# Two products of 512 and 256 columns in place of three of 256, and both halves of an input tile side by side

## The chip, the cores and the metric

The kernel runs on one core of one Trainium2 chip. The metric is the device time of one execution in microseconds (us). TensorE (PE in the rows; PEld is its weight load) multiplies matrices into PSUM banks, VectorE (DVE) and ScalarE (ACT) work on tiles elementwise, GpSimd (POOL) does little here, and SyncE (SP) issues the loads.

## What is computed

One layer of a diffusion backbone over 256 latent tokens (`x`) with 256 context tokens (`ctx`), width 2048, in float32. The part that the change touches is the modulated norm and the start of the combined input projection:

```python
qa, ka, va, qb, kb, vb, rb, gf, gb, gate_a, gate_b = proj(modulate(x, g_mix[l], mod_x[0], mod_x[1]))
cqa, cka, cva, cqb, ckb, cvb, crb, cgf, cgb, cgate_a, cgate_b = proj(
    modulate(ctx, g_mix[l], mod_c[0], mod_c[1]))

def modulate(x, g, shift, scale):
    return rms_norm(x, g) * (1 + scale) + shift
```

`proj` multiplies by `w_in` (2048 rows, 13,344 columns) and splits the columns. The 1024 columns of `qb` are wanted of the latent tokens alone; `kb` and `vb` of both. After that come gated linear attention, windowed attention, the merge and a ConvFFN, which the change leaves as they are except for where some tiles lie.

## The kernel before

**Products in three parts.** A float32 factor is split in two: `hi` is the factor rounded to the matmul's type, `lo` is the rest. A product is then the sum of three matmuls: `hi` with `hi`, `hi` with `lo`, and `lo` with `hi`. For the weights, `wsplit` loads two K tiles (256 rows) by 512 columns into `raw`, ACT writes `whi` (line 220) and DVE subtracts to get `wlo` (line 221). Three such pairs of tiles are alive at a time: a new `whi` or `wlo` waits until TensorE is done with the one three steps back. A "step" below is one such pair of K tiles.

**The input.** The 16 K tiles of the normed input (`h`) are made in five groups as the modulation arrives: `GROUPS = [(0, 2), (2, 2), (4, 4), (8, 4), (12, 4)]` (first tile, number), called group 0 to group 4 here. `affine_shift` writes `hi` with ACT and `lo` with DVE (lines 543 and 546). They lie in four tiles `h0hi` to `h3hi` and four `h0lo` to `h3lo`, each with latent and context tokens of four K tiles.

**The loop over groups** (line 650 on). For each group from group 1 on it runs four column blocks: two query blocks of 512 columns (`QB0` and `QB1` here, `proj_T`, latent tokens only), a key block (`KB`, `proj_T` over both kinds of tokens, 512 columns of `h` a product) and a value block (`VA`, `proj_nat`). Each block sums its K tiles in PSUM banks (`acc`, a pool of four) and then adds the banks to an accumulator in SBUF (`qb0`, `kb0`, `va0`) with DVE at line 555. `KB` and `VA` use four banks; a query block uses two, each with two outputs of 256 columns. A bank of the next block but one, or of the next block where that uses all four, waits until its add is done. A group has one step (group 1) or two (groups 2 to 4) for each block.

**What stands between the blocks.** In groups 1 to 3 the modulation of the next group is worked out in between: `pm` products on loads named `mraw`, a transpose on DVE (`mtr`), `pcol` products, and small DVE operations on `scale`, `shift` and `xr`. In group 4 there are none. TensorE's order is that of the program up to the end of group 3; in group 4 the scheduler orders the instructions by its own reckoning of when each is ready. After group 4 come the `plr` products of a low-rank projection, four transposes `ptr`, 16 small products `plb`, and the rest of the layer.

**Later use of the tiles.** The context halves of the eight `h` tiles hold other data later: the natural-order input, the inner results `g`, and the attention's output.

Of the kernel before, what the change touches and what calls it, by code (L numbers as in the profile page):

```python
# [32 lines left out]
def layer_kernel(ctx, tc, A, out):  # L33
# [238 lines left out]
    def proj_T(w, c0, kts, rhs, evac, mid=None, fresh=False, by_tile=False):  # L272

        wide = rhs[0] is h_both
        per = 1 if wide else 2
        banks = [acc.tile([P, 512], F32, name="acc", tag="acc") for _ in range(4 // per)]
        for k0 in kts[::2]:
# [4 lines left out]
            for part in range(2):  # L282
                if whole and part:
                    break
                if part:
                    (mid or midway)()
                todo = [(f, k, x) for f in range(4) for k in range(nk) for x in range(2 - part)]
                if fresh and part == 0:
                    todo = [(f, k, x) for x in range(2) for k in range(nk) for f in range(4)]
                if whole:  # L290
                    todo = [(f, k, x) for f in range(4) for x in range(3) for k in range(nk)]
                end = None
                for f, k, x in todo:
                    kt = k0 + k
                    low = part == 1 or x == 2
                    w_ = (lo if low else hi)[:, k, f * P:(f + 1) * P]
                    b = f % per
                    o = banks[f // per]
                    if wide:
                        o = o.rearrange("p (s t) -> p s t", s=2)  # L300
                    else:
                        o = o[:, b * T:(b + 1) * T]
                    if whole and f == 2 and x + k == 0:
                        midway()
                    i = mm(o, w_, rhs[0](kt)[x % 2], start=(kt == kts[0] and b == 0 and not low and x == 0),
                           stop=(kt == kts[-1] and low), skip_group_check=True).ins
                    if whole and end is not None:
                        in_order(end, i)
                    end = i
# [199 lines left out]
    def h_tok(s, t):  # L509
        return lambda kt: (hh[kt // 4][:, s, kt % 4, t * P:(t + 1) * P],  # L510
                           hl[kt // 4][:, s, kt % 4, t * P:(t + 1) * P])

    def h_all(s):
        return lambda kt: (hh[kt // 4][:, s, kt % 4, :], hl[kt // 4][:, s, kt % 4, :])

    def h_both(kt):
        return hh[kt // 4][:, :, kt % 4, :], hl[kt // 4][:, :, kt % 4, :]
# [20 lines left out]
    def affine_shift(s, t0, n, behind=None):  # L538
        for kt in range(t0, t0 + n):
            xk = xr[2 * s + kt // 8][:, kt % 8, :]  # L540
            sh = shift1[:, s, kt:kt + 1]
            hi, lo = hh[kt // 4][:, s, kt % 4, :], hl[kt // 4][:, s, kt % 4, :]
# [15 lines left out]
    hh, hl = [], []  # L558

    def more_h(half):  # L560
        for q in (2 * half, 2 * half + 1):
            hh.append(M(f"h{q}hi", [P, 2, 4, T], F32R))
            hl.append(M(f"h{q}lo", [P, 2, 4, T], F32R))
# [86 lines left out]
    for gi, (t0, n) in enumerate(groups):  # L650
# [40 lines left out]
        for s in range(2):  # L691
# [371 lines left out]
    def natural(step):  # L1063
        raw = fetched.pop(step)
        e = step % 2
        if step >= KT // 2:
            a = S.activation(hh[e][:, 1], raw, AF.Copy).ins
            in_order(last_hi[0], a)
            in_order(last[0], a)
            a = V.tensor_tensor(hl[e][:, 1], raw, hh[e][:, 1].bitcast(F32), op=ALU.subtract).ins  # L1070
# [12 lines left out]
        split(hh[e][:, 1], hl[e][:, 1], raw)  # L1083
# [79 lines left out]
    def all_values():  # L1163
# [3 lines left out]
        def inner(step):  # L1167
            e = step % 2
            ax, ac = pair_x[step // (KT // 2)], pair_c[step // (KT // 2)]
            hn = (hh[e][:, 1], hl[e][:, 1])  # L1170
# [10 lines left out]
            for k in range(2):  # L1181
                split(hh[2 + e][:, 1, 2 * k:2 * k + 2, :], hl[2 + e][:, 1, 2 * k:2 * k + 2, :], gb[k])

        def outer(step, i, w):
# [4 lines left out]
            gs = [g[2 + e][:, 1].rearrange("p (k h) t -> p k h t", h=2) for g in (hh, hl)]  # L1189
# [85 lines left out]
    def attend(g, qT, qr):  # L1275
        for t in range(2):
# [53 lines left out]
            split(hh[g][:, 1, :, t * P:(t + 1) * P], hl[g][:, 1, :, t * P:(t + 1) * P],  # L1330
# [65 lines left out]
    for j in range(4):  # L1396
# [6 lines left out]
        proj_nat(A["w_attn_o"][0], 0, j * 512, ALL, [h_tok(1, 0), h_tok(1, 1)], at_evac)  # L1403
# [246 lines left out]
```

## Time and profile before

| what | before |
|---|---|
| median of 3 runs (lowest, highest) | 1936.68 us (1936.21, 1939.33) |
| the profiled execution | 1936.14 us |
| its span, first to last instruction | 1934.4 us |
| TensorE busy | 99% of the span |
| VectorE, ScalarE, GpSimd busy | 75%, 52%, 3% |
| mean granted TensorE clock | 0.999 of full speed |
| DMA over the span | 232 GB/s, all 16 engines busy in the first 96 us |

The profiled execution lasts 1.7 us longer than its span and lies 0.54 us under the median. The groups 1 to 4 take the stretch from 46 to 195 us of the span. A matmul's row gives a start and a modelled duration that overlaps with the next one, so what a matmul costs in a stream is the distance of the starts.

### The profile page before, as it was taken

To read this page: it belongs to the slowest core of one execution; us is meant where nothing else is said; L and a number is where in the kernel's file an instruction comes from. 1 tells how busy PE (TensorE), PEld (TensorE's weight loads), DVE (VectorE), ACT (ScalarE), POOL (GpSimd) and SP (SyncE) were. 2 spreads that over 40 slices of the span, in tenths; PEclk is the share of its full clock that TensorE was granted. 3 is DMA by queue.
4 is the path that set the end of the run, shared out by engine and by line. 5 is a ranking of instruction groups with operands and counts; after the bars stand their busy time and mean duration, and the time that the engine had idled before them with its cause. 6 is when DMAs were issued, how large, how long until landed. Compare 5 with 4: busy or idle time off the path is not lost.

```text
span 1934.4 us, 26471 instructions
## 1 busy us (share of the span) xinstructions
PE 1918.6 (99%) x9858; PEld 1595.9 (83%) x9858; DVE 1446.8 (75%) x2241; ACT 1007.7 (52%) x1469; POOL 51.2 (3%) x81
## 2 busy tenths in 40 slices
PE   8999999999999999999999999999999999999999
PEld 6678888888888887788888888888888888888887
DVE  5656767989787767898888776998886556777654
ACT  5223566666344456655544455755565334555532
POOL 0010110000100000000000000000000000000000
PEclk9999999999999999999999999999999999999999
DMA  9985325878976764457999987688886566666663
GB/s 396 413 304 147 94 66 186 247 253 270 321 241 214 236 186 120 128 182 226 347 344 350 349 278 221 206 279 277 282 268 218 193 194 186 189 192 186 198 214 109
DMA packets 194528, 450.24 MB, mean 233 GB/s; under 512 B 13776, under 2 KB 18128, under 8 KB 188512
## 3 DMA queue, kind: packets, MB, share of 16 engines
q1 hardware_dynamic: 187568, 428.13, 67.0%
q0 software_dynamic: 2912, 10.82, 1.6%
q10 hardware_dynamic: 3920, 9.61, 1.3%
q8 instruction: 77, 1.26, 0.3%
q14 instruction: 51, 0.42, 0.1%
HBM read 435.86 MB, written 12.65 MB: 232 GB/s over the span
## 4 chain that ended last, share of the span: by engine, by line
PE 95%; DMA 3%; DVE 1%; ACT 0%; issue 0%; SPq 0%; ACTq 0%
PE acc L84 70%; PE accs L84 13%; PE pg L84 4%; PE pa L96 2%; DMA raw<-in_w_in 1%; PE poa L96 1%; PE pS L96 1%; DMA mraw<-in_w_mod 1%; PE pm L96 1%; DMA xr<-in_ctxT 1%; PE ptp L99 1%; DVE wlo L221 0%; PE pto L99 0%; DMA pack<-in_k_pack 0%; PE plr L646 0%; PE pz L96 0%
## 5 line engine op out<-in xcount | busy, mean ns | idle before, releaser
L220 ACT ACTIVATE whi<-raw 128x1024 fp32r<-128x1024 f32 x568 | 601.3, 1060 | 732.7 <-PE acc L84 501.7
L221 DVE TENSOR_TENSOR wlo<-raw,whi 128x1024 fp32r<-128x1024 f32 x568 | 693.8, 1223 | 351.2 <-ACT whi L220 328.3
L84 PE MATMUL accs<-h,whi 128*128 128x512 f32 x704 | 244.5, 392 | 0.0
L84 PE MATMUL acc<-h,whi 128*128 128x512 f32 x640 | 222.3, 392 | 0.0
L84 PE MATMUL accs<-h,wlo 128*128 128x256 f32 x704 | 196.0, 278 | 0.0
L84 PE MATMUL acc<-h,wlo 128*128 128x256 f32 x640 | 178.1, 278 | 0.0
L84 PEld LDWEIGHTS accs<-h,whi 128*128 128x128 f32 x704 | 131.8, 187 | 29.8
L84 PEld LDWEIGHTS acc<-h,whi 128*128 128x128 f32 x640 | 119.8, 187 | 27.0
L84 PE MATMUL acc<-whi,ah 128*128 128x512 f32 x352 | 137.1, 389 | 0.0
L84 PE MATMUL acc<-whi,al 128*128 128x512 f32 x352 | 137.0, 389 | 0.0
L84 PEld LDWEIGHTS accs<-h,wlo 128*128 128x128 f32 x704 | 132.6, 188 | 0.0
L84 PEld LDWEIGHTS acc<-h,wlo 128*128 128x128 f32 x640 | 120.6, 188 | 0.1
L84 PE MATMUL acc<-whi,h2hi 128*128 128x512 f32 x256 | 101.1, 395 | 0.1
L84 PE MATMUL acc<-whi,h2lo 128*128 128x512 f32 x256 | 99.9, 390 | 0.9 <-DVE h2lo L63 0.9
L84 PE MATMUL acc<-whi,th 128*128 128x512 f32 x256 | 100.5, 393 | 0.0
L84 PE MATMUL acc<-whi,h3hi 128*128 128x512 f32 x256 | 100.2, 392 | 0.0
L84 PE MATMUL acc<-whi,h3lo 128*128 128x512 f32 x256 | 99.9, 390 | 0.0
L84 PE MATMUL acc<-whi,tl 128*128 128x512 f32 x256 | 99.7, 389 | 0.0
L84 PE MATMUL acc<-wlo,ah 128*128 128x512 f32 x352 | 94.2, 389 | 0.0
L403 DVE CUSTOM_DVE_ANT_0 raw<-raw,csrow,pack 128x1024 f32<-128x1024 f32 x64 | 81.8, 1278 | 0.0
L84 PEld LDWEIGHTS acc<-wlo,ah 128*128 128x128 f32 x352 | 66.1, 188 | 13.8
L84 PEld LDWEIGHTS acc<-whi,al 128*128 128x128 f32 x352 | 66.1, 188 | 13.7
(390 smaller groups left out, 3596.7 us busy)
## 6 DMA issues: line engine op xcount, KB each, us to landing
raw<-in_w_in SPq DMA_DIRECT2D x204, 512.0 KB, 4.4
raw<-in_w_up SPq DMA_DIRECT2D x176, 512.0 KB, 4.4
raw<-in_w_modT SPq DMA_DIRECT2D x128, 512.0 KB, 4.7
raw<-in_w_down SPq DMA_DIRECT2D x88, 512.0 KB, 4.0
mraw<-in_w_mod SPq DMA_DIRECT2D x32, 1024.0 KB, 14.0
raw<-in_w_attn_o SPq DMA_DIRECT2D x32, 512.0 KB, 5.8
raw<-in_w_gla_o SPq DMA_DIRECT2D x32, 512.0 KB, 5.8
raw<-in_w_out SPq DMA_DIRECT2D x32, 512.0 KB, 5.9
```

Source lines behind the costliest of these rows:

```text
L84: r = pe_seq(PE.matmul(*a, **k))
L96: return pe_seq(after(PE.matmul(*a, **k)))
L99: return pe_seq(after(PE.transpose(*a)))
L220: j = S.activation(hi[:, 0:n, :], raw[:, 0:n, :], AF.Copy).ins
L221: i = V.tensor_tensor(lo[:, 0:n, :], raw[:, 0:n, :], hi[:, 0:n, :].bitcast(F32), op=ALU.subtract).ins
L403: i0 = V.tensor_tensor_reduce(out=raws[i], in0=raws[i], in1=row[0], scale=1.0, scalar=d if h else bmod[:, b0:b0 + 1], op0=ALU.mult, op1=AL ...
```

## The change

The eight `h` tiles now hold two K tiles each, with `hi` and `lo` of a K tile next to each other, so that 512 columns of one product can run over both (`h_pair`). In the query blocks of groups 1 to 4, `whi` is multiplied with those 512 columns at once, and `wlo` with the 256 of `hi`. An output then takes a whole bank, 256 columns for `hi` and 256 for `whi` with `lo`, so that a query block has four banks, and `q_sums` adds each bank with two DVE additions of 256 columns. Group 0 stays as it was. The later users of the context halves address them through `half_of`, in the same shapes.

```diff
     def proj_T(w, c0, kts, rhs, evac, mid=None, fresh=False, by_tile=False):
 
         wide = rhs[0] is h_both
-        per = 1 if wide else 2
+        pair = rhs[0] is h_pair
+        per = 1 if wide or pair else 2
         banks = [acc.tile([P, 512], F32, name="acc", tag="acc") for _ in range(4 // per)]
...
-                todo = [(f, k, x) for f in range(4) for k in range(nk) for x in range(2 - part)]
+                todo = [(f, k, x) for f in range(4) for k in range(nk) for x in range(1 if pair else 2 - part)]
                 if fresh and part == 0:
-                    todo = [(f, k, x) for x in range(2) for k in range(nk) for f in range(4)]
+                    todo = [(f, k, x) for x in range(1 if pair else 2) for k in range(nk) for f in range(4)]
...
-                    else:
+                    elif not pair:
                         o = o[:, b * T:(b + 1) * T]
+                    elif low:
+                        o = o[:, 0:T]
...
-                    i = mm(o, w_, rhs[0](kt)[x % 2], start=(kt == kts[0] and b == 0 and not low and x == 0),
+                    i = mm(o, w_, rhs[0](kt)[part if pair else x % 2], start=(kt == kts[0] and b == 0 and not low and x == 0),
...
+    def h_pair(kt):
+        return hp[kt // 2][:, 0, kt % 2, :, :].rearrange("p i t -> p (i t)"), hp[kt // 2][:, 0, kt % 2, 0, :]
+
+    def half_of(i, q):
+        return hp[4 * i + q][:, 1].rearrange("p k i t -> p (k i) t")
...
-    hh, hl = [], []
+    hp = []
 
     def more_h(half):
-        for q in (2 * half, 2 * half + 1):
-            hh.append(M(f"h{q}hi", [P, 2, 4, T], F32R))
-            hl.append(M(f"h{q}lo", [P, 2, 4, T], F32R))
+        for q in range(4 * half, 4 * half + 4):
+            hp.append(M(f"h{q}", [P, 2, 2, 2, T], F32R))
+
+    def q_sums(j):
+        def evac(i, b):
+            d = qb0[2 * j + i // 2][:, (i % 2) * T:(i % 2) * T + T]
+            V.tensor_tensor(d, d, b[:, 0:T], op=ALU.add)
+            V.tensor_tensor(d, d, b[:, T:2 * T], op=ALU.add)
+        return evac
...
-                    proj_T(w_in, QB + j * 512, kts, [h_all(0)], add_to(lambda i, j=j: qb0[2 * j + i], False),
+                    proj_T(w_in, QB + j * 512, kts, [h_pair], q_sums(j),
                            mid=mid if j else None, fresh=(gi == 2 and j == 0))
...
-        split(hh[e][:, 1], hl[e][:, 1], raw)
+        split(half_of(0, e), half_of(1, e), raw)
```

VectorE in group 1, around the end of the first query block: `acc_526` is the first bank of that block; `wlo_622` and `wlo_702` are the low halves of the weights of `KB` and `VA`; `acc_565` on are banks of the second query block. Before:

```order
L221 TENSOR_TENSOR wlo_568<-raw_513,whi_567 128x1024
L546 SCALAR_TENSOR_TENSOR h0lo_231<-xr2_87,shift1_101,h0hi_230 128x256
L555 TENSOR_TENSOR qb0_234<-qb0_234,acc_526 128x512
L546 SCALAR_TENSOR_TENSOR h0lo_231<-xr2_87,shift1_101,h0hi_230 128x256
L221 TENSOR_TENSOR wlo_622<-raw_515,whi_621 128x1024
L221 TENSOR_TENSOR wlo_702<-raw_517,whi_701 128x1024
L555 TENSOR_TENSOR qb0_235<-qb0_235,acc_527 128x512
L555 TENSOR_TENSOR qb0_236<-qb0_236,acc_565 128x512
```

And now, where `acc_526` to `acc_529` are the first block's four banks:

```order
L557 SCALAR_TENSOR_TENSOR h1_231<-xr2_87,shift1_101,h1_231 128x256
L578 TENSOR_TENSOR qb0_234<-qb0_234,acc_526 128x256
L579 TENSOR_TENSOR qb0_234<-qb0_234,acc_526 128x256
L221 TENSOR_TENSOR wlo_622<-raw_515,whi_621 128x1024
L221 TENSOR_TENSOR wlo_702<-raw_517,whi_701 128x1024
L578 TENSOR_TENSOR qb0_234<-qb0_234,acc_527 128x256
L578 TENSOR_TENSOR qb0_235<-qb0_235,acc_528 128x256
L579 TENSOR_TENSOR qb0_234<-qb0_234,acc_527 128x256
L579 TENSOR_TENSOR qb0_235<-qb0_235,acc_528 128x256
L578 TENSOR_TENSOR qb0_235<-qb0_235,acc_529 128x256
L579 TENSOR_TENSOR qb0_235<-qb0_235,acc_529 128x256
```

The adds of three of the four banks stand behind the two subtractions for later blocks.

VectorE in group 4, from the end of `VA` of group 3 to the first adds of the second query block. Before, `acc_1479` and `acc_1480` are the banks of `QB0`, `acc_1543` one of `QB1`; `wlo_1578`, `wlo_1627`, `wlo_1657` and `wlo_1695` are the low weights of the second step of `QB1`, the two steps of `KB` and the first of `VA`:

```order
L555 TENSOR_TENSOR va0_108<-va0_108,acc_1394 128x512
L221 TENSOR_TENSOR wlo_1578<-raw_1575,whi_1577 128x1024
L555 TENSOR_TENSOR qb0_234<-qb0_234,acc_1479 128x512
L221 TENSOR_TENSOR wlo_1627<-raw_1624,whi_1626 128x1024
L555 TENSOR_TENSOR qb0_235<-qb0_235,acc_1480 128x512
L221 TENSOR_TENSOR wlo_1657<-raw_1654,whi_1656 128x1024
L555 TENSOR_TENSOR qb0_236<-qb0_236,acc_1543 128x512
L555 TENSOR_TENSOR qb0_237<-qb0_237,acc_1544 128x512
L221 TENSOR_TENSOR wlo_1695<-raw_1692,whi_1694 128x1024
```

Now `acc_1447` to `acc_1450` are the banks of `QB0`, `acc_1503` the first of `QB1`; the same four low weights are `wlo_1532`, `wlo_1579`, `wlo_1609` and `wlo_1647`:

```order
L221 TENSOR_TENSOR wlo_1532<-raw_1529,whi_1531 128x1024
L578 TENSOR_TENSOR qb0_234<-qb0_234,acc_1447 128x256
L221 TENSOR_TENSOR wlo_1579<-raw_1576,whi_1578 128x1024
L579 TENSOR_TENSOR qb0_234<-qb0_234,acc_1447 128x256
L578 TENSOR_TENSOR qb0_234<-qb0_234,acc_1448 128x256
...
L579 TENSOR_TENSOR qb0_235<-qb0_235,acc_1450 128x256
L781 TENSOR_TENSOR wgl_1753<-wtm_1744,wgl_1753 64x1024
L221 TENSOR_TENSOR wlo_1609<-raw_1606,whi_1608 128x1024
L578 TENSOR_TENSOR qb0_236<-qb0_236,acc_1503 128x256
L221 TENSOR_TENSOR wlo_1647<-raw_1644,whi_1646 128x1024
L579 TENSOR_TENSOR qb0_236<-qb0_236,acc_1503 128x256
```

The two adds of the first bank of each block now have a weight subtraction between them, and `wgl` stands ahead of the adds of `QB1`.

TensorE in group 4, from the last products of `QB0` into `QB1`. Before, each `whi` product of 256 columns with `h3hi` alternates with one with `h3lo`:

```order
L84 MATMUL acc_1480<-h3hi_1106,whi_1513 128x256
L84 MATMUL acc_1480<-h3lo_1107,whi_1513 128x256
L84 MATMUL acc_1479<-h3hi_1106,wlo_1514 128x256 x4
L84 MATMUL acc_1480<-h3hi_1106,wlo_1514 128x256 x4
L84 MATMUL acc_1543<-h3hi_1106,whi_1547 128x256
L84 MATMUL acc_1543<-h3lo_1107,whi_1547 128x256
```

And now, where `h6_1090` and `h7_1091` hold the four K tiles of group 4, two each:

```order
L84 MATMUL acc_1450<-h7_1091,wlo_1476 128x256 x2
L99 MATMUL ptr_1726<-pack_81,rrow_167 128x128 x2
L99 MATMUL ptr_1726<-pack_81,rrow_393 128x128 x2
L788 MATMUL plb_1756<-shift1_101,wlr_523 32x2 x16
L84 MATMUL acc_1503<-h6_1090,whi_1509 128x512 x2
L84 MATMUL acc_1503<-h6_1090,wlo_1510 128x256 x2
L84 MATMUL acc_1503<-h7_1091,whi_1531 128x512 x2
L84 MATMUL acc_1503<-h7_1091,wlo_1532 128x256
L84 MATMUL acc_1504<-h6_1090,whi_1509 128x512 x2
L84 MATMUL acc_1505<-h6_1090,whi_1509 128x512 x2
```

`ptr` and `plb` moved here from behind `plr`, and the products of a block no longer come step by step, but bank by bank in part. ScalarE's reads of `ptr` and `plb` moved with them, ahead of its `whi` for the second step of `KB`. In groups 2 and 3, where VectorE had eight `xr` multiplications between the adds of `QB1` and the next `wlo`, six stand there now and two behind that `wlo`. SP's and GpSimd's order is unchanged, and behind this stretch all engines have the order of before.

## Rows read from the trace of the kernel before

**Rows 1.** The page, part 4: the chain that ended last, by engine.

```profile
PE 95%; DMA 3%; DVE 1%; ACT 0%; issue 0%; SPq 0%; ACTq 0%
```

**Rows 2.** TensorE's waits, whole span: us in total, times, longest us.

```profile
PE warm L572 <- DMA pack<-in_k_pack: 6.2, 1, 6.2
PE pm L96 <- DMA mraw<-in_w_mod: 2.8, 4, 1.0
PE acc L84 <- DVE h2lo L63: 0.9, 1, 0.9
...
```

**Rows 3.** Timeline of group 4: start us, duration us, what.

```profile
161.50 0.28 PE L84 MATMUL acc<-h3hi,whi 128*128 128x256 f32 x1
...
163.41 1.12 PE L84 MATMUL acc<-h3hi,wlo 128*128 128x256 f32 x8
...
178.48 0.39 PE L84 MATMUL acc<-h3hi,whi 128*128 128x512 f32 x1
...
182.10 1.98 PE L84 MATMUL acc<-h3hi,wlo 128*128 128x512 f32 x8
```

**Rows 4.** VectorE's groups by form: count | busy us, mean ns | idle before.

```profile
L1531 DVE TENSOR_TENSOR us<-acc,us 128x256 f32<-128x256 f32 x44 | 16.5, 414 | 0.0
...
L555 DVE TENSOR_TENSOR kb<-kb,acc 128x512 f32<-128x512 f32 x16 | 10.1, 681 | 7.6 <-PE acc L84 7.6
```

**Rows 5.** Timeline of group 1.

```profile
47.27 1.06 ACT L628 ACTIVATE va<-acc 128x512 f32<-128x512 f32 x2
...
49.54 1.07 PE L96 MATMUL pm<-mraw,cS 128*32 128x512 f32 x8
...
50.17 2.35 DVE L221 TENSOR_TENSOR wlo<-raw,whi 128x1024 fp32r<-128x1024 f32 x2
...
52.64 1.92 PE L96 MATMUL pm<-mraw,cS 128*32 128x512 f32 x16
...
56.01 1.06 PE L96 MATMUL pm<-mraw,cS 128*32 128x512 f32 x8 [0.30 <-DMA mraw<-in_w_mod]
...
63.46 1.07 PE L96 MATMUL pm<-mraw,cS 128*32 128x512 f32 x8 [0.64 <-DMA mraw<-in_w_mod]
...
65.41 2.47 DVE L555 TENSOR_TENSOR kb<-kb,acc 128x512 f32<-128x512 f32 x4
```

**Rows 6.** Timeline of the start of group 2.

```profile
74.56 1.22 PE L84 MATMUL acc<-h1hi,whi 128*128 128x256 f32 x8
...
75.27 1.28 DVE L555 TENSOR_TENSOR va<-va,acc 128x512 f32<-128x512 f32 x2
```

**Rows 7.** Timeline from QB1 to KB, in group 2 and (last row) group 3.

```profile
89.99 1.22 PE L84 MATMUL acc<-h1hi,wlo 128*128 128x256 f32 x8
...
92.27 3.26 DVE L534 SCALAR_TENSOR_TENSOR xr<-xr,scale,rrow 128x256 f32<-128x256 f32 x8
...
95.44 3.49 DVE L221 TENSOR_TENSOR wlo<-raw,whi 128x1024 fp32r<-128x1024 f32 x3
...
96.75 2.08 PE L84 MATMUL acc<-h1hi,wlo 128*128 128x512 f32 x8
...
141.61 1.67 PEld L84 LDWEIGHTS acc<-h2hi,wlo 128*128 128x128 f32 x8 [0.26 <-DVE wlo L221]
```

**Rows 8.** Timeline of group 4 and what follows it.

```profile
163.66 1.06 ACT L220 ACTIVATE whi<-raw 128x1024 fp32r<-128x1024 f32 x1 [2.67 <-PE acc L84]
...
167.25 0.28 PE L84 MATMUL acc<-h3hi,whi 128*128 128x256 f32 x1
...
173.01 0.40 PE L84 MATMUL acc<-h3hi,whi 128*128 128x512 f32 x1
...
196.75 0.66 PE L99 MATMUL ptr<-pack,rrow 128*128 128x128 f32 x4
...
197.70 0.50 PE L84 MATMUL acc<-h0hi,whi 128*128 128x512 f32 x1
```

**Rows 9.** Windows view, 36 to 40 us: busy us of PE, PEld, DVE, ACT, POOL; granted clock.

```profile
36.00:40.00 4.00, 2.24 (x33) 1.49 (x26) 3.35 (x9) 1.53 (x4) 0.00 (x0) 1.00 1.01 394
```

More of the change, by code (lines that the diff above doesn't have):

```diff
@@ L509, in h_tok, with h_att @@
     def h_tok(s, t):
-        return lambda kt: (hh[kt // 4][:, s, kt % 4, t * P:(t + 1) * P],
-                           hl[kt // 4][:, s, kt % 4, t * P:(t + 1) * P])
+        return lambda kt: tuple(hp[kt // 2][:, s, kt % 2, i, t * P:(t + 1) * P] for i in range(2))
     def h_all(s):
-        return lambda kt: (hh[kt // 4][:, s, kt % 4, :], hl[kt // 4][:, s, kt % 4, :])
+        return lambda kt: tuple(hp[kt // 2][:, s, kt % 2, i, :] for i in range(2))
     def h_both(kt):
-        return hh[kt // 4][:, :, kt % 4, :], hl[kt // 4][:, :, kt % 4, :]
+        return tuple(hp[kt // 2][:, :, kt % 2, i, :] for i in range(2))
+    def h_pair(kt):
+        return hp[kt // 2][:, 0, kt % 2, :, :].rearrange("p i t -> p (i t)"), hp[kt // 2][:, 0, kt % 2, 0, :]
+    def half_of(i, q):
+        return hp[4 * i + q][:, 1].rearrange("p k i t -> p (k i) t")
+    def h_att(t):
+        return lambda kt: tuple(half_of(i, kt // 4)[:, kt % 4, t * P:(t + 1) * P] for i in range(2))
     h_x = [h_tok(0, 0), h_tok(0, 1)]
@@ L541, in affine_shift @@
             sh = shift1[:, s, kt:kt + 1]
-            hi, lo = hh[kt // 4][:, s, kt % 4, :], hl[kt // 4][:, s, kt % 4, :]
+            hi, lo = h_all(s)(kt)
             j = S.activation(hi, xk, AF.Identity, bias=sh).ins
@@ L1066, in natural @@
         if step >= KT // 2:
-            a = S.activation(hh[e][:, 1], raw, AF.Copy).ins
+            a = S.activation(half_of(0, e), raw, AF.Copy).ins
             in_order(last_hi[0], a)
             in_order(last[0], a)
-            a = V.tensor_tensor(hl[e][:, 1], raw, hh[e][:, 1].bitcast(F32), op=ALU.subtract).ins
+            a = V.tensor_tensor(half_of(1, e), raw, half_of(0, e).bitcast(F32), op=ALU.subtract).ins
             in_order(last_lo[0], a)
@@ L1169, in inner @@
             ax, ac = pair_x[step // (KT // 2)], pair_c[step // (KT // 2)]
-            hn = (hh[e][:, 1], hl[e][:, 1])
+            hn = (half_of(0, e), half_of(1, e))
             gb = [bank("pg", (P, 2, T), side=True) for _ in range(2)]
@@ L1181, in inner @@
             for k in range(2):
-                split(hh[2 + e][:, 1, 2 * k:2 * k + 2, :], hl[2 + e][:, 1, 2 * k:2 * k + 2, :], gb[k])
+                split(half_of(0, 2 + e)[:, 2 * k:2 * k + 2, :], half_of(1, 2 + e)[:, 2 * k:2 * k + 2, :], gb[k])
         def outer(step, i, w):
@@ L1188, in outer @@
             hi, lo = w
-            gs = [g[2 + e][:, 1].rearrange("p (k h) t -> p k h t", h=2) for g in (hh, hl)]
+            gs = [half_of(i, 2 + e).rearrange("p (k h) t -> p k h t", h=2) for i in range(2)]
             def part0(t):
@@ L1329, in attend @@
             values(*ready)
-            split(hh[g][:, 1, :, t * P:(t + 1) * P], hl[g][:, 1, :, t * P:(t + 1) * P],
+            split(half_of(0, g)[:, :, t * P:(t + 1) * P], half_of(1, g)[:, :, t * P:(t + 1) * P],
                   po.rearrange("p (a b) -> p a b", a=4))
@@ L1401, in at_evac @@
             V.tensor_tensor(a1[t], b, a1[t], op=ALU.mult)
-        proj_nat(A["w_attn_o"][0], 0, j * 512, ALL, [h_tok(1, 0), h_tok(1, 1)], at_evac)
+        proj_nat(A["w_attn_o"][0], 0, j * 512, ALL, [h_att(0), h_att(1)], at_evac)
         def mg_evac(t, b, j=j, a1=a1, a2=a2):
```

## The prediction

> **What bounds the kernel now.** I read the chain that ended last first: 95% of it is TensorE [rows 1], so the span is the sum of what TensorE executes and of its waits. The list of waits [rows 2] shows how little waiting there is: 6.2 us for the first load, 2.8 us in four waits for `mraw` early on, and behind group 1 one wait of 0.9 us. So a wait that the change adds behind group 1 is hardly given back, and a product that it shortens is earned in full. I then read the timelines of the blocks in groups 1 to 4 for two things: what a product costs, and how far ahead of TensorE the other engines are when a block begins.
>
> **The products.** In a stream, 16 products of 256 columns start from 161.50 to 163.41 us, 1.91 us or 119 ns each; 16 of 512 columns take from 178.48 to 182.10 us, 3.62 us or 226 ns each [rows 3]. A step of a query block had 16 `whi` products of 256 columns and has eight of 512 now: 1.91 against 1.81 us. The `wlo` products stay. Group 1 has one step for each query block, groups 2 to 4 two; with two query blocks that is 14 steps of 0.10 us: **-1.4 us**. The weight loads run beside the products and are in these distances already. The number of columns does not change, which is why the gain is so small.
>
> The Trainium skill (page "TensorE: Matmul & The Clock Gate", section "Back-to-back issue gap") gives a gap of N/2.4 ns plus about 2.5 ns at full clock. Estimated from that formula, the 14 steps would save 0.3 us and the sum below would be 1.1 us higher, 1944.6. The rows show 119 and 226 ns where the formula has 109 and 216.
>
> **The adds.** VectorE's add of 512 columns lasts 681 ns [rows 4], and four in a row 2.47 us [rows 5], so they start 0.60 us apart, 0.08 less than they last. An add of 256 columns out of PSUM lasts 414 ns [rows 4]; by the same overlap I take 0.33 us from start to start. A query block had two adds (1.28 us) and has eight: 7 x 0.33 + 0.41 = 2.7 us. Bounds: 3.3 us without overlap, 2.4 us at half the distance of the wide add. VectorE itself has room for this. What costs is that a query block takes all four banks now, so that each block waits for the adds of the one before it; the change has no work of its own to cover that.
>
> **Group 1.** QB0's third and fourth bank come from the block that ScalarE empties until 48.33 us [rows 5], which holds QB0 back by half a microsecond, to about 49.8; `pm` follows until 50.8. In VectorE's order the adds of three of its banks stand behind two `wlo`. These ran from 50.17 to 52.52 [rows 5] and now end at about 52.7, 0.2 later for the second short add ahead of them. The second bank is then free at 53.8 (two adds at 0.33, one of 0.41), the fourth at 54.8. TensorE does the first bank's two products until 51.3 and waits; it ends the eight at 55.3, where before the next `pm` began at 52.64 [rows 5]: 2.7 us late. The waits of 0.30 and 0.64 us for `mraw` behind it [rows 5] go, since these loads are on their way by then: 1.7 us are left, or **+1.9 us** with the 0.2 us for its two steps counted above. If the loads slipped too it would be 2.8.
>
> **Start of group 2.** QB0 here goes over the banks first and the K tiles second. It used the first two banks of VA, and VA's last two adds end at 75.95 and 76.55 us [rows 6], long after its start at 74.56. Now its third product needs the third bank, at 75.0: it starts at 76.0, the fourth at 76.6, and with five at 0.23 the eight end at 77.7. The sixteen ended at 76.6 (0.1 for the first, then 119 ns each). That is 1.15 us, **+1.25 us** without the step's gain. Group 3 has `plr` and `pm` products ahead of QB0 and I take nothing there.
>
> **QB0 to QB1 in groups 2 and 3.** Sixteen `pm` rows (1.92 us, as in [rows 5]) stand between. The adds begin some 0.6 us before the block's end and end 2.1 us after it; the bank that QB1 wants first is free by then. Behind the adds come `mtr`, which waits for the same `pm`, and QB1's `wlo`: about 0.2 us late. **+0.4 us** for both, between 0 and 1.6.
>
> **QB1 to KB in groups 2 and 3.** KB's low products start at 96.75 us, with the end of the first of three `wlo` that start at 95.44; in group 3 there is already a wait for it [rows 7]. Ahead of that `wlo` the adds take 1.4 us more, and two of eight `xr` (3.26 us for eight [rows 7], 0.4 each) move behind it: 0.6 us late in each group, **+1.2 us**, between 0 and 2.4.
>
> **Group 4.** No `pm` covers anything here. ScalarE's `whi` for QB1's second step started at 163.66, right behind the `whi` products of QB0's first step [rows 8], which ended with the start of `wlo` at 163.41 [rows 3]. In the new order the last of these products comes behind most of the second step's, at about 164.95. So that `whi` runs from 165.2 to 166.3 and its `wlo` to 167.5; the first add of QB0's first bank follows, then the `wlo` of KB, to 169.0, and only then the second add, to 169.4. TensorE is through with QB0 at 167.05 (before, QB1 began at 167.25 [rows 8]) and with `ptr` and `plb` at 168.0. These two took 0.95 us from 196.75 to 197.70 [rows 8] and are only moved. It waits 1.4 us. QB1 then runs to 174.95 without a wait, since its order takes what is ready. The same happens at its end: its first step's last `whi` product is at 172.4; ScalarE makes the next two `whi` until 173.7 and 175.4; VectorE's two `wlo` end at 174.95 and 176.65 with one add between them, and the second add at 177.0. KB starts at 177.05 in place of 173.01 [rows 8], a wait of 2.1 us. **+3.5 us**. Bounds: nothing, if the conversions keep their lead, and 5 us with slower adds.
>
> **The rest** costs nothing that I can find: the users of `half_of` issue the same operations in the same shapes, SP's order of loads is the same, and the adds of KB and VA are untouched.
>
> **Sum.** 1.9 + 1.25 + 0.4 + 1.2 + 3.5 = 8.25 us of waits, less 1.4 us of products: +6.85 us. On the profiled execution's 1936.14 us that is 1943.0; the median lies 0.54 us higher, so I predict **1943.5 us**, 0.35% slower. A measurement of this kernel tells about 0.2%, 3.9 us, from no change.
>
> **Rivals.**
> - Not slower: in group 4 the bank-by-bank order covers the waits. For it speaks that this order puts ready products wherever a bank is missing, and `ptr` and `plb` between the blocks; against it, that the second add of the first bank stands behind a `wlo` that waits for ScalarE, which waits for TensorE. Without these 3.5 us the time is 1940.0, +3.35 us, inside the 0.2%. In general this side is reached once all waits together stay under 5.3 us.
> - The change only earns its products: 1936.68 - 1.4 = 1935.3 us, also inside the 0.2%. This needs every bank to be empty in time, which the adds at 75.27 us [rows 6] exclude in group 2 at least. For a gain of over 0.2% I find no source.
> - The waits cost TensorE its clock: it is at 2.4 GHz throughout, also in a stretch with 1.76 of 4 us idle [rows 9]. The gap in group 1 is longer, about 2.5 us in one piece. If it fell to 1.2 GHz, the 24 products of a query block's step (2.8 us) would take twice as long: +2.8 us behind one gap, 1946.3, and 1951.8 behind all three. The Trainium skill (same page, section "HAM oscillation — how this bites in real kernels") says that idle gaps between bursts of products bring the lower clock back, which is this rival; [rows 9] shows a gap that did not.
> - The adds do not overlap: +0.6 us at each of the four block ends in groups 2 and 3 and about 0.8 in the rest, 1946.7. The forecast's range takes this in.
>
> **Chances.** The forecast with its own range of 1940.6 to 1947 has 0.68, the clock 0.05: slower 0.73. Fewer waits, the first two rivals, 0.22: same. Something that I do not see, on the fast side: 0.05. The range of 8 in 10 reaches into the first rival, 1938.6, and up to the slower adds, 1947.2.
>
> **What would show it.** In the profile after: 512-column products of `acc<-h` 226 ns apart in the query blocks; TensorE waiting for VectorE's `qb` adds, about 2.5 us in group 1, 1 us at the start of group 2, and 1.4 and 2.1 us in group 4; `ptr` near 167 us; from 200 us on the old timeline, some 7 us later. I am wrong if TensorE shows no wait for `qb` adds (the order covers them), if a granted clock under 1 appears between 46 and 180 us, or if waits after group 4 differ.

## The result and the profile after

The changed kernel takes 1950.3 us (median of 4 runs, 1948.27 to 1951.83), the kernel before, run beside it, 1936.53 us. The ratio is 1.0069, with a 95% interval of 1.0057 to 1.0081: some 13.4 us slower by the ratio, 13.8 between the medians. The prediction was 1943.5 us with a range up to 1947.2: the sign was right, the size was half of what came, and the measured time lies above the range.

The profiled execution took 1951.83 us, the longest of the four; its span is 1950.1 us, 15.7 us longer than that of before. The four runs took 1951.83, 1951.60, 1949.01 and 1948.27 us at a mean granted clock of 0.996, 0.996, 0.997 and 0.999, so what the clock costs differs from run to run (0.001 of it is some 2 us). TensorE's waits in it, which answer to [rows 2] (us in total, times, longest us):

```profile
PE warm L589 <- DMA pack<-in_k_pack: 6.4, 1, 6.4
PE acc L84 <- DVE qb L579: 5.7, 3, 2.2
PE pm L96 <- DMA mraw<-in_w_mod: 2.7, 4, 1.0
PE acc L84 <- ACT h L62: 2.2, 1, 2.2
PE acc L84 <- DVE wlo L221: 0.9, 2, 0.5
PE acc L84 <- DVE h L63: 0.9, 1, 0.9
PE acc L84 <- ACT h L554: 0.8, 1, 0.8
PE acc L84 <- DVE va L566: 0.7, 1, 0.7
PE acc L84 <- ACT va L645: 0.2, 1, 0.2
```

Five rows are new. `qb`, `wlo`, `va` (twice) are the waits of the prediction. The 2.2 us for `h` on ScalarE (fourth row) lie far behind group 4 and stand in no sum of mine. The two waits for `mraw` in group 1 [rows 5] are gone, as predicted; the four that are left lie between 11 and 38 us. The places of the new waits, in timelines of the same trace (start us, duration us, what, and in brackets the idle time before and its releaser): group 1, the start of group 2, KB in group 3, QB1 and KB in group 4.

```profile
55.62 2.15 PE L84 MATMUL acc<-h,whi 128*128 128x512 f32 x6 [2.22 <-DVE qb L579]
...
81.15 2.02 PE L84 MATMUL acc<-h,whi 128*128 128x512 f32 x6 [0.71 <-DVE va L566]
...
149.05 2.11 PE L84 MATMUL acc<-h,wlo 128*128 128x512 f32 x8 [0.46 <-DVE wlo L221]
...
176.99 0.69 PE L84 MATMUL acc<-h,whi 128*128 128x512 f32 x2 [1.43 <-DVE qb L579]
...
184.86 1.16 PE L84 MATMUL acc<-h,whi 128*128 128x512 f32 x4 [2.05 <-DVE qb L579]
```

With 0.47 us in group 2 and 0.23 us in group 1, these make 7.6 us. VectorE at two of these places, ahead of the wait of 2.22 us and of that of 1.43 us:

```profile
52.12 2.35 DVE L221 TENSOR_TENSOR wlo<-raw,whi 128x1024 fp32r<-128x1024 f32 x2
54.39 0.75 DVE L578 TENSOR_TENSOR qb<-qb,acc 128x256 f32<-128x256 f32 x2
55.06 0.74 DVE L579 TENSOR_TENSOR qb<-qb,acc 128x256 f32<-128x256 f32 x2
...
174.96 0.41 DVE L578 TENSOR_TENSOR qb<-qb,acc 128x256 f32<-128x256 f32 x1
175.29 1.22 DVE L221 TENSOR_TENSOR wlo<-raw,whi 128x1024 fp32r<-128x1024 f32 x1
176.43 0.41 DVE L579 TENSOR_TENSOR qb<-qb,acc 128x256 f32<-128x256 f32 x1
```

The adds stand behind subtractions for later blocks, as the prediction had it. The view of windows (busy us of PE, PEld, DVE, ACT, POOL; granted clock; DMA) shows what I had not counted on:

```profile
36.00:40.00 4.00, 2.24 (x35) 1.30 (x24) 3.17 (x9) 1.72 (x4) 0.00 (x0) 0.98 1.01 394
40.00:44.00 4.00, 4.00 (x30) 3.03 (x29) 2.75 (x11) 0.00 (x0) 0.00 (x0) 0.59 1.07 393
...
56.00:60.00 4.00, 4.00 (x18) 1.24 (x20) 0.55 (x2) 0.00 (x0) 0.00 (x0) 0.61 1.02 426
60.00:64.00 4.00, 4.00 (x28) 2.03 (x21) 2.63 (x8) 0.00 (x0) 0.00 (x0) 0.96 0.99 405
...
532.00:536.00 4.00, 0.96 (x4) 0.41 (x3) 2.10 (x3) 2.03 (x3) 0.00 (x0) 0.85 0.45 150
536.00:540.00 4.00, 4.00 (x10) 3.13 (x11) 3.48 (x7) 1.86 (x2) 0.00 (x0) 0.50 0.65 237
540.00:544.00 4.00, 4.00 (x15) 3.21 (x15) 4.00 (x7) 0.63 (x2) 0.00 (x0) 0.80 0.57 170
```

In the kernel before, all of these windows have 1.00, as this one:

```profile
56.00:60.00 4.00, 3.99 (x21) 2.66 (x22) 1.27 (x2) 0.00 (x0) 0.00 (x0) 1.00 1.01 422
```

A granted clock of 0.50 is the lower level, 1.2 GHz; values between are mixtures of the two. TensorE falls to it in three places: in group 0, whose products the change leaves as they were; right behind the gap in group 1; and right behind the new wait near 530 us. The fall in group 0 comes behind the very stretch of [rows 9]: TensorE is busy for the same 2.24 us of it in both kernels. A busy window of 4 us at 0.6 does the work of 2.4 us at full speed. So the first costs 1.6 us, the second 1.7 us (0.39 and 0.04 of 4 us), the third 2.8 us in the last two windows and some 0.5 in the first: 6.6 us in all.

The wait near 530 us, in rows of SP's queue, ScalarE and TensorE:

```profile
524.94 0.38 SPq L105 DMA_DIRECT2D raw<-in_w_in  x1
...
532.81 1.06 ACT L220 ACTIVATE whi<-raw 128x1024 fp32r<-128x1024 f32 x1 [6.71 <-DMA raw<-in_w_in]
533.77 1.07 ACT L62 ACTIVATE h<-pg 128x512 fp32r<-128x512 f32 x2
...
534.40 0.50 PE L84 MATMUL acc<-whi,h 128*128 128x512 f32 x1 [2.17 <-ACT h L62]
```

A weight load is issued at 524.94 us and lands at 532.8, 7.8 us later; the same load took 6.3 us in the kernel before (513.19 to 519.53). ScalarE has its `whi` ahead of the split of `pg`, so that split, which has all it needs, stands behind the load, and TensorE behind the split. The wait of 0.9 us for `h` on VectorE, right behind, is that of [rows 2]; the 2.17 us are new.

### The profile page after: what moved, and what is told of

The parts are those of the page before. It is cut to its first block, busy times and chain, and to the rows that moved or that the text cites. A ratio compares the mean times of both kernels' runs of the same rounds, so it can differ in the third digit from the quotient of the medians.

```text
span 1950.1 us, 26320 instructions
## 1 busy us (share of the span) xinstructions
PE 1924.8 (99%) x9746; PEld 1592.0 (82%) x9746; DVE 1458.5 (75%) x2289; ACT 1008.4 (52%) x1469; POOL 51.3 (3%) x81
## 3 DMA queue, kind: packets, MB, share of 16 engines
q8 instruction: 76, 1.25, 0.3%
## 4 chain that ended last, share of the span: by engine, by line
PE 94%; DMA 3%; DVE 2%; ACT 1%; issue 0%; SPq 0%; ACTq 0%; DVEq 0%
PE acc L84 70%; PE accs L84 13%; PE pg L84 4%; PE pa L96 2%; DMA raw<-in_w_in 1%; PE poa L96 1%; PE pS L96 1%; PE pm L96 1%; DVE wlo L221 1%; PE ptp L99 1%; DMA mraw<-in_w_mod 1%; ACT whi L220 0%; PE pto L99 0%; DMA dh<-raw 0%; DVE xr L545 0%
## 5 line engine op out<-in xcount | busy, mean ns | idle before, releaser
L84 PE MATMUL acc<-whi,h 128*128 128x512 f32 x1792 | 452.9, 393 | 3.0 <-ACT h L62 2.2
L84 PEld LDWEIGHTS acc<-whi,h 128*128 128x128 f32 x1792 | 334.7, 189 | 72.8 <-ACT h L62 2.6
L84 PE MATMUL acc<-h,whi 128*128 128x512 f32 (+1 forms) x1056 | 323.3, 390 | 7.5 <-DVE qb L579 5.7
L84 PE MATMUL acc<-wlo,h 128*128 128x512 f32 x896 | 244.6, 393 | 0.0
L84 PEld LDWEIGHTS acc<-h,whi 128*128 128x128 f32 x1056 | 192.2, 189 | 61.9 <-issue 16.0
L84 PE MATMUL acc<-h,wlo 128*128 128x256 f32 (+1 forms) x904 | 230.7, 295 | 0.9 <-DVE wlo L221 0.9
L84 PEld LDWEIGHTS acc<-wlo,h 128*128 128x128 f32 x896 | 167.0, 189 | 33.7
L84 PEld LDWEIGHTS acc<-h,wlo 128*128 128x128 f32 x904 | 162.2, 188 | 10.8 <-DVE wlo L221 2.5
L84 PEld LDWEIGHTS acc<-whi,ah 128*128 128x128 f32 x352 | 66.1, 188 | 13.7
```

Of the source, the lines that this page charges most:

```text
L84: r = pe_seq(PE.matmul(*a, **k))
```

## The experiments

My theory (1): the bank adds make TensorE wait as predicted, two of the gaps cost TensorE's clock on top, and the lateness meets a late load near 530 us. Rivals: the new layout costs something itself (2); the merged products cost something (3); lateness of TensorE costs more than itself, whatever it comes from (4); the clock fell by chance and not for the gaps (5). "Before" below is the kernel before, run beside each.

**The layout alone.** The query blocks of groups 1 to 4 (the text on record says 2 to 4) are back at three products of 256 columns, in the new tiles:

```diff
-                    proj_T(w_in, QB + j * 512, kts, [h_pair], q_sums(j),
+                    proj_T(w_in, QB + j * 512, kts, [h_all(0)], add_to(lambda i, j=j: qb0[2 * j + i], False),
```

> The changed kernel with its query blocks of groups 2 to 4 back at three products of 256 columns and adds of a whole bank; the paired layout of the tiles stays. Theory 1 (the waits for the bank adds, the clock lost behind one of them, and a late load that the lateness brings make up the whole loss): the layout is free, so the time is that of the kernel before, 1936 to 1938 us. The rival (the paired layout itself costs, in splits or in the order of the adds): half of the loss or more stays, 1943 us or above.

Measured: 1937.46 us (10 runs), before 1936.91 (16 runs), ratio 1.0002 (0.9993 to 1.0011). As expected by theory 1, the layout costs nothing that these runs can tell (at most 2 us by the interval); rival 2 falls.

**Two halves of two banks.** The merged products stay, but a query block runs as two halves of two banks each, over both steps, with `ptr` and `plb` in their old place:

```diff
+    def proj_halves(w, c0, kts, evac, mid=None):
+        steps = []
+        for half in range(2):
+            banks = [acc.tile([P, 512], F32, name="acc", tag="acc") for _ in range(2)]
...
-                    proj_T(w_in, QB + j * 512, kts, [h_pair], q_sums(j),
-                           mid=mid if j else None, fresh=(gi == 2 and j == 0))
+                    proj_halves(w_in, QB + j * 512, kts, q_sums(j), mid=mid if j else None)
```

> The merged products of 512 and 256 columns stay, but each query block is run in two halves of two banks, so that two banks are being added while two are filled, and ptr and plb stay at their old place. Theory 1: the bank waits in groups 1, 2, 3 and 4 are gone (below 0.5 us each), with them the clock dip at 56 to 60 us, and only the shorter products are left: 1935 to 1937 us, 13 to 15 us below the changed kernel. The rival (the merged products themselves cost): above 1940 us.

Measured: 1942.78 us (7 runs), before 1936.91, ratio 1.0028 (1.0017 to 1.0039): a miss. It wins a little over half of the loss back. Group 4 lost its waits, but in group 1 VectorE keeps two `wlo` ahead of QB0's adds (50.36 to 52.63 us), so 2.15 us of the gap stay there, and three new waits for `wlo` (2.3 us) come in groups 2 and 3, as I read it because a half block wants its low weights earlier. The clock falls behind that gap (0.86 and 0.72) and behind a wait of 1.38 us near 530 us (0.66 and 0.91). Two banks of slack don't help where the adds queue behind other work.

**The gap in group 1 closed.** VectorE's order in group 1: the `wlo` of KB and VA behind QB0's adds. `hold` lists what each coming `wlo` has to stand behind, `q_last` is the last add of a query block.

```diff
+            q_last[:] = [V.tensor_tensor(d, d, b[:, T:2 * T], op=ALU.add).ins]
...
+                    if gi == 1 and j == 0:
+                        hold[1:2] = [[hold[1], q_last[0]], q_last[0]]
```

> The changed kernel, but in group 1 the wlo splits of KB and VA are held on DVE behind the adds of QB0's banks. One gap alone is taken away. Theory 1: the 2.2 us wait at 55.6 us falls below 1 us and the granted clock stays at 1.00 from 56 to 60 us: 1.5 us (gap alone) to 3.5 us (gap and clock) below the changed kernel, 1947 to 1949 us. The rival (the clock there does not hang on the gap): the gap closes, but a clock under 1 stays in 50 to 65 us, and at most 1.5 us comes back.

Measured: 1945.47 us (4 runs), before 1936.91, ratio 1.0042 (1.0027 to 1.0057). QB1 in the timeline, then the window behind it:

```profile
51.13 2.51 PE L84 MATMUL acc<-h,whi 128*128 128x512 f32 x8
```

```profile
56.00:60.00 4.00, 4.00 (x25) 2.59 (x24) 3.33 (x9) 0.00 (x0) 0.00 (x0) 1.00 1.02 418
```

The row no longer carries a wait, the clock stays at 1.00, and 4.8 us come back between the medians where the gap itself was 2.2. That is more than the 1.5 to 3.5 us expected; one ground may be group 0, where this trace has no dip (a fall of the clock) either. Near 530 us it still waits (1.53 us) and loses clock (0.82 and 0.75 in two windows). The eight products take 2.44 us, to the next `pm` at 53.57, where 8 x 226 ns [rows 3] make 1.81. That fits short waits for banks inside the row, since QB0's adds run until 52.8 us; the list of waits shows none of them.

**The gaps in group 4 closed too.** The same kernel, with this as well:

```diff
+                    if gi == 4:
+                        hold[:] = [None, q_last[0]]
```

> The kernel with QB0's adds first in group 1, and now in group 4 too: the wlo of QB1's second step is held on DVE behind all adds of QB0, the wlo of KB's second step behind all adds of QB1. Theory 1 (the two waits in group 4 are the 3.5 us they show, and each us of lateness before the state stage also feeds the wait for a load near 530 us): the waits of 1.4 and 2.1 us fall below 0.5 us each, and the time is 3 to 6 us below the kernel with group 1's order alone, 1939.5 to 1942.5 us. The rival (what DVE puts off there comes back as a wait for wlo): at most 1.5 us below it.

Measured: 1940.96 us (10 runs, 1939.11 to 1945.07), before 1936.93, ratio 1.0020 (1.0011 to 1.0030). The waits of 1.43 and 2.05 us are now none and 0.34 us, and 4.5 us come back for 3.1 us of waits, as expected. In its trace, that of the shortest of the ten runs, the wait near 530 us is 0.33 us, and the clock stays at 1.00 up to the last microseconds.

**Fillers in the gaps.** The changed kernel with transposes without use where TensorE idles; they are meant to shorten no wait.

```diff
+    def fill(n, b):
+        i = last[0]
+        for _ in range(n):
+            k = pe_seq(PE.transpose(b[:, 0:P], ident, ident)).ins
+            in_order(i, k)
+            i = k
+        last[0] = i
...
+                    if gi == 1 and j:
+                        fill(18, pl)
...
+                if step == 1:
+                    fill(14, bank("late"))
```

> The changed kernel with filler on TensorE where it stands still: 18 transposes of 128x128 without use ahead of QB1 of group 1, 14 ahead of the first product that waits near 530 us (with the weight load late). No wait is shortened by it. If the clock loss behind these waits is a cost of its own, the granted clock stays at 1.00 behind both, and 4 to 5 us of the two dips come back: 1944.5 to 1947.5 us. If the dips come from something else (the gap only coincides with them), they stay and the time is that of the changed kernel, 1948 to 1952 us.

Measured: 1945.37 us (4 runs), before 1936.93, ratio 1.0047 (1.0030 to 1.0064). The filler in group 1 and the rest of the gap in the timeline, then the window where the clock had fallen:

```profile
51.56 2.19 PE L661 MATMUL plr<-pack 128*128 128x128 f32 x18
...
54.51 1.82 PE L84 MATMUL acc<-h,whi 128*128 128x512 f32 x6 [0.30 <-DVE qb L579]
```

```profile
56.00:60.00 4.00, 4.00 (x34) 1.58 (x32) 1.34 (x5) 0.00 (x0) 0.00 (x0) 1.00 1.01 418
```

In group 1 the delay is the same: QB1's third product starts 2.95 us behind the start of the filler, and it started 2.96 us behind QB1's first product without one (52.66 and 55.62 us). The clock stays at 1.00, and from that third product to the start of group 2 TensorE takes 22.46 us (54.51 to 76.97) in place of 24.09 (55.62 to 79.71). These 1.6 us are what the windows say that the clock cost there. So idle time of TensorE cost more than itself, and rival 5 falls for group 1.

Near 530 us the test is weaker than planned, because the load landed earlier in this trace. TensorE comes to the filler at 528.68 us, and ScalarE begins the split of `pg` at 529.39. In the changed kernel the waiting product starts 0.63 us behind the start of that split (533.77 and 534.40), and two products of 0.61 us stand ahead of it; without the filler the wait here would thus have been about 0.7 us (an estimate from these rows), not 2.17.

Between the medians (1950.3 and 1945.37) the kernel is 4.9 us faster. That holds the clock of group 1, but also a shorter wait near 530 us that the filler did not bring about, and this trace has no dip in group 0. What is left over before, 8.4 us, is near the price of the waits without the clock; I had predicted 6.85.

The two fillers apart:

> The changed kernel with the 18 useless transposes ahead of QB1 of group 1 alone; nothing fills the wait near 530 us. If each gap costs its own clock: the clock stays at 1.00 from 46 to 64 us, some 2 us of the 4.9 us that both fillers gave come back, 1947 to 1949 us, and the wait near 530 us still shows a clock under 1 behind it when it is over 1 us long. If the clock near 530 us hangs on what happened in group 1, both dips go and the time is that with both fillers, 1945 to 1946 us.

> The changed kernel with the 14 useless transposes near 530 us alone. The gap of 2.2 us in group 1 stays. If each gap costs its own clock: a clock under 1 in 56 to 62 us as in the changed kernel, none near 530 us, and 1946.5 to 1948.5 us, 2 to 3 us below the changed kernel. If that of group 1 came by chance in the one execution that was traced, no dip there, and 1945 to 1946 us.

Measured: 1946.47 us with the filler in group 1 alone, 1947.19 us with the one near 530 us alone (4 runs each), before 1936.51; ratios 1.0049 (1.0033 to 1.0066) and 1.0057 (1.0042 to 1.0072). Filler in group 1 only, group 4's stretch:

```profile
184.00:188.00 4.00, 4.00 (x13) 3.12 (x12) 0.00 (x0) 0.57 (x2) 0.00 (x0) 0.66 0.22 80
```

Filler near 530 us only, groups 0 and 1:

```profile
40.00:44.00 4.00, 4.00 (x31) 3.05 (x29) 2.77 (x11) 0.00 (x0) 0.00 (x0) 0.60 1.07 395
...
56.00:60.00 4.00, 4.00 (x18) 1.34 (x20) 0.56 (x2) 0.00 (x0) 0.00 (x0) 0.60 1.02 424
```

The medians are 3.8 and 3.1 us below the changed kernel; the first is half a microsecond below the range expected, the second inside it. Group 1's dip is gone with its filler and comes back, with the same 0.60, when only that filler is left out, so it is no chance of one trace. Near 530 us neither trace decides. Without a filler there the wait was 0.97 us and cost no clock; with one, the load landed so early (the split starts at 531.50 us, the filler at 531.48) that hardly any wait was left to fill. The runs of either kernel spread over 4 us, and 3.8 and 3.1 are together more than the 4.9 of both fillers, so four runs do not price one filler. The 2.05 us gap of group 4 cost clock with the filler in group 1 alone, though it had not in the changed kernel.

**Lateness without a gap.** The kernel before with transposes without use behind `plr` of group 4, 58 (6.3 us, from 196.8 to 203.1) or 116 (12.6 us); and 58 of them behind the stretch near 530 us:

```diff
+    late = bank("late", side=True)
+    i = last[0]
+    for _ in range(58):
+        j = PE.transpose(late[:, 0:P], ident, ident).ins
+        in_order(i, j)
+        i = j
+    last[0] = i
```

> The kernel before with 58 transposes of 128x128 without use on TensorE behind group 4's plr, some 7 us of its work; nothing else is changed, and TensorE does not stand still there. If lateness is handed on one to one, the time is 7 us above the kernel before, 1943 to 1944 us. If lateness ahead of the state stage costs more than itself (the load of the next weights lands later still, TensorE waits some 2 us for it at about 530 us and loses clock behind that wait), 9 to 13 us above: 1945.5 to 1949.5 us, with a wait on ScalarE's h near 530 us and a granted clock of 0.5 to 0.7 behind it.

> The kernel before with the same 58 useless transposes, but behind the whole state stage's value products instead of behind group 4. If the extra over 7 us of the first delay came from the wait for the load near 530 us, there is no such wait and no clock under 1 here, and the time is 6.5 to 7.2 us above the kernel before, 1943.3 to 1944.2 us. If any 7 us of lateness cost more than itself: 1944.6 us or above, as with the delay behind group 4.

> The kernel before with 116 useless transposes behind group 4's plr, 14 us instead of 7. If the wait for the load near 530 us grows with the lateness (1.25 us at 6.3 us late, 2.17 us at 11 us late in the changed kernel): a wait of 2.5 to 3 us there and a clock dip behind it, 16 to 19 us above the kernel before, 1953 to 1956 us. If it stays as with 7 us: 14.5 to 15.5 us above, 1951.5 to 1952.5 us.

Measured: 1944.6 us, 7.7 over before, between my two readings (4 runs; 1.0044, 1.0027 to 1.0060); behind 530 us 1943.54, 6.6 over, as the first reading has it (5 runs; 1.0036, 1.0023 to 1.0049); double 1949.47, 12.5 over (4 runs; 1.0065, 1.0050 to 1.0080). The double one is a miss of both readings that I gave it: I had put the transposes at 120 ns where they take 109, and its wait near 530 us is not longer but shorter. The first trace has a wait of 1.25 us there with a clock of 0.77 and 0.80 behind it, the double one 0.87 us and none:

```profile
528.62 0.49 PE L84 MATMUL acc<-whi,h2hi 128*128 128x512 f32 x1 [1.25 <-ACT h2hi L62]
```

```profile
534.93 0.50 PE L84 MATMUL acc<-whi,h2hi 128*128 128x512 f32 x1 [0.87 <-ACT h2hi L62]
```

So lateness is carried to the end about one to one, and rival 4 falls as a rule: the wait near 530 us does not grow with it. The three traces that come to that stretch on time (before, the layout alone, the delay behind it) wait 0, 0.35 and 0.47 us there; those that come late wait between 0 and 2.17 us, in no order of their lateness.

**A gap alone.** The kernel before, with TensorE held ahead of QB1 of group 1 by six small adds on GpSimd; then with 18, and with 38 transposes ahead of the one that waits.

```diff
...
+                    if gi == 1 and j:
+                        d = qb0[0]
+                        G.tensor_tensor(slow, d[:, 0:P], d[:, P:T], op=ALU.add)
+                        for q in range(5):
+                            G.tensor_tensor(slow, slow, d[:, 0:P], op=ALU.add)
+                        i = last[0]
+                        for x in [ident] * 0 + [slow]:
+                            k = pe_seq(PE.transpose(pl[:, 0:P], x, ident)).ins
...
```

(`* 18` and `* 38` in place of `* 0` in the other two.)

> The kernel before, with TensorE made to stand still ahead of QB1 of group 1: one transpose without use there waits for six small adds without use on GpSimd, which start when QB0's first bank is added. About 2 us of idle TensorE at the place where the changed kernel has its 2.2 us, everything else as before. If idle time there costs TensorE's clock: a granted clock of 0.5 to 0.8 in the 4 us behind the gap, and 3 to 4.5 us above the kernel before, 1939.5 to 1941.5 us. If a gap costs itself alone (and part of it goes into the later waits of 0.3 and 0.6 us for mraw): 1 to 2 us above, 1938 to 1939 us, and the clock stays at 1.00.

> The same, with 18 transposes of 128x128 without use ahead of the one that waits, so that TensorE works through the time that it idles in the kernel with the gap. The later start of QB1 is the same. By the first theory the clock stays at 1.00 and 1.5 to 2.5 us of the gap's cost come back: 1938 to 1939 us. By the second the two kernels take the same time.

> The kernel before, with the same 4.4 us delay ahead of QB1 of group 1 as in the two kernels with the gap, but all of it filled: 38 useless transposes ahead of the one that waits. If the typical 5.3 us of the half-filled kernel hold clock lost in the 2.3 us left idle, 3.3 to 4 us above the kernel before, 1939.6 to 1940.5 us. If they are lateness that grows on its way (later loads), 5 us above as when half filled, 1941 to 1942 us.

The gap came out at 4.41 us instead of 2, since GpSimd's adds took 0.86 us each. Measured over before: 5.9 us empty (7 runs; 1.0031, 1.0019 to 1.0042), 5.3 us half filled (8 runs; 1.0027, 1.0017 to 1.0037), 4.3 us filled (9 runs; 1.0025, 1.0015 to 1.0035). The times alone do not show the clock: the empty gap, twice as long as planned, lies above both readings; empty and half filled take about the same time, as the second reading had it; and the filled one lies between its two. The traces do tell the clock apart. The empty gap in the timeline and the window behind it, then the same window half filled (2.29 us idle are left there):

```profile
55.12 0.47 PE L709 MATMUL plr<-pack,slow 128*128 128x128 f32 x1 [4.41 <-POOL slow L706]
```

```profile
56.00:60.00 4.00, 4.00 (x23) 3.11 (x25) 0.00 (x0) 0.00 (x0) 0.00 (x0) 0.50 1.02 418
```

```profile
56.00:60.00 4.00, 4.00 (x35) 2.43 (x34) 0.06 (x1) 0.00 (x0) 0.00 (x0) 1.00 1.01 420
```

In the traces the `plr` behind group 4 start at 200.86 us with the empty gap, at 198.38 half filled and at 198.41 filled: 2.5 us of clock for the empty gap, and none for the 2.29 us left idle. Over before, the medians are only 0.6 us apart from empty to half filled, and 1.6 us from empty to filled, less than that. The traced run of the empty gap was its longest and that of the half filled one its shortest. The mean granted clock of the other runs is known (0.998 or 0.999 empty, 0.998 to 1.000 in the two others), but with some 2 us to each 0.001 it does not say what they lost. So that the gap costs clock is shown here in one trace of each kernel, and not by the times.

**Both orders mended and 5 transposes ahead of the wait near 530 us.**

> The kernel with the adds first in groups 1 and 4, and 5 transposes without use ahead of the product that waits near 530 us. If what that kernel still loses in some of its runs is clock behind that wait: 1937.5 to 1939.5 us, within 0.2% of the kernel before, with less spread than the 1939 to 1945 us seen without the filler. If its spread has other grounds: 1940 to 1942 us, as without. It is not expected to beat the kernel before: the merged products give back under 1 us.

Measured: 1940.9 us (8 runs, 1939.77 to 1943.06), before 1936.30; 1.0024 (1.0014 to 1.0035). The second reading came out: the filler gives nothing over the 1940.96 us without it. Its trace, of the longest of the eight runs, has the dip in group 0 (0.57 from 40 to 44 us), a wait of 1.29 us near 530 us, and none of the clock lost behind it. No version beats the kernel before.

## Why the prediction was wrong, and what of it held

**The waits were right.** Predicted and shown: group 1 about 2.5 and 2.22 us; the start of group 2 3.14 us from its first product to its low ones and 3.30 (79.71 to 83.01), of which 0.71 are listed as a wait; QB1 to KB 0.6 in each group and 0.47 and 0.46; group 4 1.4 and 2.1 against 1.43 and 2.05. Only the 0.4 us between QB0 and QB1 in groups 2 and 3 do not appear in the list. In group 4 the second add of the first bank did stand behind a `wlo`; closing that gap and the one in group 1 by VectorE's order alone took 9.3 us off (1950.3 to 1940.96), more than the waits themselves.

**The products** earn a little less than I said. A first step of QB0 in group 3, from its first product to its low ones, after and then before:

```profile
126.41 2.12 PE L84 MATMUL acc<-h,whi 128*128 128x512 f32 x8
128.36 0.88 PE L84 MATMUL acc<-h,wlo 128*128 128x256 f32 x6
```

```profile
119.44 0.39 PE L84 MATMUL acc<-h2hi,whi 128*128 128x256 f32 x1
...
121.46 0.76 PE L84 MATMUL acc<-h2hi,wlo 128*128 128x256 f32 x5
```

1.95 against 2.02 us, 0.07 instead of 0.10. If all 14 steps are like this one, that is 1.0 instead of 1.4 us, but earned: rival 3 falls. The kernel with both fillers, whose trace has no clock loss and a short wait near 530 us, came out 8.4 us slower (1945.37 us), inside my range.

**The step that failed** is that the sum puts the clock behind the waits at nothing; in the profiled execution it cost 6.6 us. I gave the rival "The waits cost TensorE its clock" 0.05, on the ground that a stretch with 1.76 of 4 us idle had kept the clock at 1.00 [rows 9]. I had read that stretch as one gap. It holds two waits, of 0.92 and 0.84 us, and it does not always keep the clock: in the changed kernel the same stretch, with waits of 0.99 and 0.77 us, was followed by 0.59. One trace was too little evidence. Group 1's gap took the clock in all three traces that had it unfilled (2.22, 2.22 and, with the half blocks, 2.15 us), and I had myself named a clock under 1 between 46 and 180 us as what would prove me wrong. The size in that place was 1.7 us, below the 2.8 us of the rival. That the rival's 1951.8 us for all three gaps comes near the measured 1950.3 is luck: the two gaps of group 4 kept the clock in the profiled execution, and it was lost in group 0 and near 530 us instead, where the rival had nothing.

The page of the Trainium skill that I cited then, "TensorE: Matmul & The Clock Gate", has a second section that bears on this, "A second HAM failure mode: psum-queue depth-cycling": in a kernel that goes round the PSUM banks in each iteration, frequent short idle times of TensorE between groups of products make the clock swing between its two levels. The traces agree that a short wait for a bank can bring the lower clock, 0.61 behind 2.22 us and 1.00 with the same time filled; here one such wait was enough.

**What I left out** is the second thing that the sum puts at nothing: I wrote that from 200 us on everything would only be some 7 us later, and that I would be wrong if waits after group 4 differ. They do. The wait near 530 us was 2.17 us in the profiled run, with 3.3 us of clock behind it. The clock behind it was lost in four traces with a wait of 1.25 to 2.17 us and no filler, and in none with 1.14 us or less. That the load is late is seen; which lateness makes it land late is not settled, since 6.3 us of pure delay showed 1.25 us there and 12.6 us showed 0.87.

**The sum of the profiled execution**, by places. The same products behind group 4, before and after:

```profile
199.08 1.07 PE L779 MATMUL plr<-lrp,pack 128*32 128x512 f32 x8
```

```profile
210.04 1.06 PE L796 MATMUL plr<-lrp,pack 128*32 128x512 f32 x8
```

They are 11.0 us late where I had said 7. Group 1 already begins 1.7 us late (48.15 against 46.47 us), which is the clock lost in group 0. The clock in group 1 makes another 1.7 us, and 7.6 us are left for the waits less the products in groups 1 to 4, against my 6.85. From there to the end 4.7 us more are lost; the wait near 530 us and the clock behind it make 5.5, so that 0.8 us come back in places that I did not look for.

**Open.** The dip in group 0 (1.6 us) stands in three of the nine traces with the paired tiles and in none of the seven with the old ones, with the same 1.76 us of idle time ahead of it in all; I can't say if it belongs to the change. That the wait near 530 us brings the clock loss behind it is read off the traces and not tested: no pair of kernels has the same wait there with and without filler. The fourth run of the changed kernel (1948.27 us) has a mean clock of 0.999, that of before, and still lies above my range; no trace says why. And the kernel with both orders mended stays 4 us over before in the median where its trace shows 2.9.

## What to carry to other kernels

When TensorE bounds a kernel, price a new wait of one or two microseconds twice: once as itself, and once as the clock that it may lose behind it; work without use in the gap tells the two apart, if the trace shows that the gap was still there to fill. A product that is merged to save issue distance takes more PSUM, and with it the slack that let the adds queue behind other work; look up what stands ahead of those adds on the adding engine first, since changing that order gave back most of the loss here.

## What the runs showed of the hardware

- A gap's length alone did not decide on the clock. 2.05 us in group 4, with 1.43 us of idle time that ended 5.8 us ahead of it, left it at 1.00 in four traces and brought 0.66 in one; 2.22 us in group 1 brought 0.61 and 0.60 in its two traces; 2.29 us behind 2.2 us of filler brought nothing.
- The same two waits in group 0, 1.76 us together, left the clock at 1.00 in 13 traces and brought 0.57 to 0.60 in three.
- Transposes of 128x128 without use, 109 ns apart, held the clock at 1.00: 12.6 us of them in a row, and 18 in place of a gap that cost clock without them.
- GpSimd's add of 128x128 took 0.86 us when five ran in a row (4.31 us, and TensorE's wait for them ended with them).
